# A feed-forward up-projection by seven block products, with the gated activations kept in DRAM until a separate down-projection

## The chip, the cores and the metric

One core of a Trainium2 chip runs one encoder layer (token mixer, cross attention, gated feed-forward network) on 2048 tokens of width 1024. The metric is the device time of one execution in microseconds (us), and runs are compared by their median. TensorE (PE) multiplies matrices into PSUM, VectorE (DVE), ScalarE (ACT) and GpSimd (POOL) work on elements, and SyncE (SP) issues the DMAs. Each engine takes its instructions in the order of the program and waits on semaphores for the others.

## The reference, cut to what matters

```python
def conv_glu_ffn(h, w_up, conv_w, conv_b, w_down):
    u = h @ w_up
    gate, val = u[..., :D_FF], u[..., D_FF:]
    gate = causal_dwconv(gate, conv_w, conv_b)
    return (jax.nn.silu(gate) * val) @ w_down

x = x + mem_cross_attn(h, memn, x_wq[l], x_wkv[l], x_wo[l])
h = rmsnorm(x, norm_ffn[l])
x = x + conv_glu_ffn(h, f_up[l], f_conv_w[l], f_conv_b[l], f_down[l])
return rmsnorm(x, norm_final)
```

`D_FF` is 2816. The convolution runs along the tokens and has three taps. All arrays are fp32.

## The kernel before, in words

After the token mixer comes a block in which a scheduler sets the order of each engine's instructions. It works on two halves of 1024 tokens, and each half is two blocks of 512 tokens (`NB` = 2, `TB` = 512). For a half: `out_proj` and `scores` for both blocks, then `attn_out` for both, which leaves the residual `x` and the scaled operand `h3` of eight tiles (128 rows of the model width by 512 tokens) in SBUF, then `ffn`.

An fp32 product is made of three matmuls. A value is split into a high part (a cast to the rounded type fp32r, on ScalarE) and a low part (value minus high part, on GpSimd or VectorE), and a product is high x high, high x low and low x high. So each raw weight tile costs one cast and one subtraction per 512 columns before it can be used. `load_w` does that into `whl`, from the two buffers of `wraw`.

`ffn` loops over `f`, the 22 tiles of 128 feed-forward rows. For each `f` it multiplies the gate weights with `h3` of both token blocks (24 matmuls each), applies the scale of the normalization (`bc3`), the three taps (ScalarE's L1385 and twice L1387 on VectorE) and the activation (L1390, L1391, L1392), then does the same with the value weights, multiplies (L1398) and splits the result into `act`. After every second `f` (`GRP`), it multiplies the two `act` tiles of each block with the down weights and adds to the residual in SBUF (L1417). After the last `f` of a half comes the final normalization (`finish`). `ahead` puts the next half's first `out_proj` before the last down-projection group.

The buffers that matter: `kt` has 32 tiles of 128x1024 (4 KB a row), `kq` 7 of the same size, `T` 6 and `TQ` 4 of 128x512, PSUM 7 banks (`PD`). A buffer is taken again when its last reader is done.

Of the kernel before, what the change touches and what calls it, by code (L numbers as in the profile page):

```python
# [13 lines left out]
F32 = mybir.dt.float32  # L14
# [42 lines left out]
def tile_hybrid_encoder(ctx: ExitStack, tc: tile.TileContext, t_in: dict, out: bass.AP, stage: str = "all"):  # L57
# [1132 lines left out]
    x1_dram = dram.tile([KT, P, S], F32, name="x1_dram")  # L1190
    align(tp, 320)
# [133 lines left out]
    def attn_out(s_, between):  # L1325
        x2, h3, acc = [], [], None
        for d in range(KT):
            w = [pre_split(vo_dram[d, q], (P, 2, 4, P), "wvo") for q in range(2)]
            w = [(t_[:, 0], t_[:, 1]) for t_ in w]
            if d % 2 == 0:  # L1330
                xx = K4((P, 2, TB), "x2", F32)
            x = xx[:, d % 2, :]
# [16 lines left out]

    def attention(st, toks):  # L1350
        pr = None
        for b in range(NB):
# [14 lines left out]
    GRP = 2  # L1367

    def ffn(tok0, st, xs, h3, ahead):
        acts = [[] for _ in range(NB)]  # L1370
        wds = []
        for f in range(NFF):
            wg = load_w(t_in["f_up"][f])
            us = []
            for b in range(NB):
                ps = PD()
                dense(ps, wg, h3[b])
                if f == 0 and b == 0:
                    norm_bc(st[NB - 1])
                    bc3 = [s_["bc3"] for s_ in st]  # L1380
                gt_ = T((P, TB + 2), "gt_")
                nc.gpsimd.tensor_copy(gt_[:, 0:2], fcar[f])
                nc.vector.tensor_tensor(gt_[:, 2:], ps, bc3[b], ALU.mult)
                u = T(name="fu")
# [8 lines left out]
                us.append(u)  # L1393
            wv = load_w(t_in["f_up"][NFF + f])
            for b in range(NB):
                ps = PD()
                dense(ps, wv, h3[b])
                nc.vector.scalar_tensor_tensor(us[b], us[b], 0.5, ps, ALU.mult, ALU.mult)  # L1398
                a = K4((P, 2, TB), "act")
                split_sbuf(a[:, 0, :], a[:, 1, :], us[b])  # L1400
                acts[b].append(a)
            wds.append(split_w(load_raw(t_in["f_down"][f]), [P, 8, P], kq, ("kq", "kq"), 7))
            if f == NFF - 1:
                ahead()
            if len(wds) == GRP:
                end = f == NFF - 1
                bcf = []
                order = [(d, b) for b in range(NB) for d in range(KT)] if end else [(d, b) for d in range(KT) for b in range(NB)]
                for d, b in order:
                    ps = PD(name="dps")  # L1410
                    for g in range(GRP):
                        a = acts[b][g]
                        hi, lo = wds[g]
                        nc.tensor.matmul(ps, hi[:, d, :], a[:, 0, :], start=(g == 0), stop=False)  # L1414
                        nc.tensor.matmul(ps, hi[:, d, :], a[:, 1, :], start=False, stop=False)  # L1415
                        nc.tensor.matmul(ps, lo[:, d, :], a[:, 0, :], start=False, stop=(g == GRP - 1))  # L1416
# [126 lines left out]
```

## Time and profile before

| | |
|---|---|
| median of 3 runs | 3452.25 us (3449.77 to 3452.82) |
| the profiled execution: time, span | 3447.24 us, 3445.5 us |
| PE busy | 3321.1 us (96%), 17388 matmuls |
| DVE, ACT, POOL busy | 1902.4, 1170.9, 1177.1 us (55, 34, 34%) |
| mean granted TensorE clock | 0.987 |
| chain that ended last: PE, DVE, DMA | 80, 9, 3% |

The span runs from the first to the last instruction. Matmuls overlap, so the pitch of a matmul is read from starts, not from its own length of 389 ns. A row of the timeline gives start, length, engine, line, operation, output and inputs, how many instructions it merges, and in brackets the idle time before it and what ended it.

### The profile page before, as it was taken

The numbers are of one execution on the slowest core, as the hardware profiler recorded it, in microseconds if no ns is written. First come the engines' busy times: TensorE is split into PE (matmuls) and PEld (weight loads), VectorE is DVE, ScalarE is ACT, GpSimd is POOL, SyncE is SP. The second block draws the span as 40 slices with busy tenths as digits, with TensorE's granted clock in tenths as the row PEclk, the third lists the DMA queues.
The fourth block names the chain that finished last, engine by engine and source line by source line (L and its number), as shares of the span: only waits on it lengthen the run. The fifth ranks groups of instructions, "written<-read, shape, count | busy, mean of one in ns | idle before, by whom it ended". The sixth has DMA issues, their size and how long they took to land.

```text
span 3445.5 us, 47020 instructions
## 1 busy us (share of the span) xinstructions
PE 3321.1 (96%) x17388; PEld 2728.8 (79%) x17388; DVE 1902.4 (55%) x3916; ACT 1170.9 (34%) x2307; POOL 1177.1 (34%) x1254
## 2 busy tenths in 40 slices
PE   6899999999999989899999999999999999999997
PEld 4777787788778778688888888887888888888886
DVE  5887777777777775343244444444643344444445
ACT  5445433543443345442221221222432212212213
POOL 5333121211211123531343443444531434434433
PEclk9999999999999999999999999999999999999998
DMA  6555444544444447766411111112656211111111
GB/s 208 207 181 180 142 142 129 178 133 137 147 130 133 131 127 242 261 208 205 139 58 40 49 55 43 44 55 95 223 178 227 96 37 56 55 37 52 53 43 55
DMA packets 225701, 423.19 MB, mean 123 GB/s; under 512 B 79552, under 2 KB 111424, under 8 KB 225472
## 3 DMA queue, kind: packets, MB, share of 16 engines
q1 hardware_dynamic: 221248, 418.10, 36.9%
q8 instruction: 137, 2.24, 0.3%
q10 hardware_dynamic: 4224, 2.10, 0.2%
q14 instruction: 92, 0.75, 0.1%
HBM read 342.44 MB, written 77.66 MB: 122 GB/s over the span
## 4 chain that ended last, share of the span: by engine, by line
PE 80%; DVE 9%; DMA 3%; ACT 3%; issue 3%; POOL 2%; SPq 0%; DVEq 0%; ACTq 0%; POOLq 0%
PE pd L173 13%; PE pd L176 12%; PE pd L175 12%; PE pd L147 12%; PE dps L1416 4%; PE dps L1415 4%; PE dps L1414 4%; PE qy L147 2%; PE sc L1295 2%; PE sc L1297 2%; PE sc L1296 2%; DVE pr L719 1%; PE pab L147 1%; DVE pr L739 1%; PE p L147 1%
## 5 line engine op out<-in xcount | busy, mean ns | idle before, releaser
L147 PE MATMUL pd<-hA,whl 128*128 128x512 f32 x2976 | 813.0, 410 | 17.1 <-ACT whl L121 8.4
L147 PEld LDWEIGHTS pd<-hA,whl 128*128 128x128 f32 x2976 | 534.8, 191 | 120.8 <-ACT whl L121 9.4
L176 PE MATMUL pd<-h,whl 128*128 128x512 f32 x1408 | 547.9, 389 | 0.0
L173 PE MATMUL pd<-h,whl 128*128 128x512 f32 x1408 | 547.9, 389 | 0.0
L175 PE MATMUL pd<-h,whl 128*128 128x512 f32 x1408 | 547.7, 389 | 0.0
L124 POOL TENSOR_TENSOR whl<-wraw,whl 128x512 fp32r<-128x512 f32 x313 | 417.5, 1345 | 327.6 <-ACT whl L121 318.8
L1417 DVE TENSOR_TENSOR x<-dps,x 128x512 f32<-128x512 f32 x352 | 235.6, 689 | 224.3 <-PE dps L1416 222.3
L121 ACT CAST whl<-wraw 128x512 fp32r<-128x512 f32 x334 | 204.0, 621 | 317.8 <-PE pd L176 271.8
L175 PEld LDWEIGHTS pd<-h,whl 128*128 128x128 f32 x1408 | 264.3, 188 | 54.9
L176 PEld LDWEIGHTS pd<-h,whl 128*128 128x128 f32 x1408 | 264.3, 188 | 54.8
L173 PEld LDWEIGHTS pd<-h,whl 128*128 128x128 f32 x1408 | 264.3, 188 | 54.8
L1416 PE MATMUL dps<-act,wlo 128*128 128x512 f32 x704 | 271.0, 390 | 0.0
L1415 PE MATMUL dps<-act,whi 128*128 128x512 f32 x704 | 270.6, 389 | 0.0
L1414 PE MATMUL dps<-act,whi 128*128 128x512 f32 x704 | 260.9, 389 | 0.1
L1398 DVE SCALAR_TENSOR_TENSOR fu<-fu,pd 128x512 f32<-128x512 f32 x88 | 60.6, 688 | 217.3 <-PE pd L176 169.8
L1414 PEld LDWEIGHTS dps<-act,whi 128*128 128x128 f32 x704 | 132.1, 188 | 28.2 <-DVE x L1417 0.8
L1415 PEld LDWEIGHTS dps<-act,whi 128*128 128x128 f32 x704 | 132.2, 188 | 27.5
L1416 PEld LDWEIGHTS dps<-act,wlo 128*128 128x128 f32 x704 | 132.2, 188 | 27.4
L1217 POOL TENSOR_TENSOR sq<-sq 128x512 f32<-128x512 f32 x56 | 73.4, 1311 | 220.6 <-ACT sq L1214 220.6
L1392 POOL TENSOR_TENSOR fu<-fu,bcs 128x512 f32<-128x512 f32 x88 | 114.2, 1298 | 97.2 <-DVE fu L1391 95.7
L1391 DVE SCALAR_TENSOR_TENSOR fu<-fth,fu 128x512 f32<-128x512 f32 x88 | 87.9, 998 | 67.6 <-ACT fth L1390 67.6
L147 PE MATMUL qy<-UV,F 128*66 128x64 f32 (+1 forms) x1024 | 124.1, 244 | 0.0
(918 smaller groups left out, 6082.8 us busy)
## 6 DMA issues: line engine op xcount, KB each, us to landing
whl<-w_split SPq DMA_DIRECT2D x186, 512.0 KB
wraw<-f_up SPq DMA_DIRECT2D x88, 512.0 KB
wqk<-qk_dram SPq DMA_DIRECT2D x64, 512.0 KB
wvo<-vo_dram SPq DMA_DIRECT2D x64, 512.0 KB
w_split<-whl SPq DMA_DIRECT2D x62, 512.0 KB
wraw<-f_down SPq DMA_DIRECT2D x44, 512.0 KB
wraw<-w_out SPq DMA_DIRECT2D x32, 512.0 KB
wraw<-w_in SPq DMA_DIRECT2D x31, 512.0 KB
```

The source lines that it names most:

```text
L121: nc.scalar.copy(t_[:, 0], r_)
L124: (nc.vector if dve else nc.gpsimd).tensor_tensor(t_[:, 1], r_, t_[:, 0].bitcast(F32), ALU.subtract)
L147: nc.tensor.matmul(out_, lhsT, rhs, **kw)
L173: nc.tensor.matmul(ps, hi[:, k % 4, :], a[:, 0, :n], start=(k == 0), stop=False)
L175: nc.tensor.matmul(ps, hi[:, k % 4, :], a[:, 1, :n], start=False, stop=False)
L176: nc.tensor.matmul(ps, lo[:, k % 4, :], a[:, 0, :n], start=False, stop=(k == last and not late))
L1391: nc.vector.scalar_tensor_tensor(u, th, 1.0, u, ALU.add, ALU.mult)
L1392: nc.gpsimd.tensor_tensor(u, u, bc3[b], ALU.mult)
L1414: nc.tensor.matmul(ps, hi[:, d, :], a[:, 0, :], start=(g == 0), stop=False)
L1415: nc.tensor.matmul(ps, hi[:, d, :], a[:, 1, :], start=False, stop=False)
L1416: nc.tensor.matmul(ps, lo[:, d, :], a[:, 0, :], start=False, stop=(g == GRP - 1))
L1417: nc.vector.tensor_tensor(xs[b][d], ps, xs[b][d], ALU.add)
```

## The change

The up-projection of one `f` is a product of 2x2 blocks: rows are gate and value weights, the inner dimension is two halves of the model width (g1, g2, v1, v2), columns are the two token blocks. Eight block products of 12 matmuls become seven. For that, the weights are combined (s1 = v1 + v2, s2 = s1 - g1, s3 = v1 - g1, s4 = g2 - s2) and so are the operands (t1 to t4, once per half), all before they are split, and the products are combined after (u2, p7, c21). The gated result is written to `act_dram`. A separate `ffn_down` then reads it back, splits it, and sums all 22 `f` in PSUM for four output tiles at a time; `f_down` is read per token block. The residual goes through `x2_dram`.

```diff
+    def resplit(t_, eng, raw=None):
+        raw = t_[:, 1].bitcast(F32) if raw is None else raw
+        nc.scalar.copy(t_[:, 0], raw)
+        eng.tensor_tensor(t_[:, 1], raw, t_[:, 0].bitcast(F32), ALU.subtract)
...
+    def attn_out(s_, o, B, between):
...
+            nc.sync.dma_start(x2_dram[d, :, s_["tok"]], x)
...
+                nc.vector.tensor_tensor(t2r, b22r, t1r, ALU.subtract)
+                nc.vector.scalar_tensor_tensor(t3r, xl, gl, b22r, ALU.mult, ALU.subtract)
+                for n, r_ in (("t1", t1r), ("t3", t3r), ("t2", t2r), ("22", b22r)):
+                    B[n].append(K4((P, 2, TB), "h3"))
+                    resplit(B[n][-1], nc.vector if n in ("t1", "t3") else nc.gpsimd, r_)
...
+    def ffn_up(hf, st, B):
...
+            a11 = plain(whl("a11"), g1, nc.gpsimd)
+            s1, s3, s2, s4 = [KQ((P, 2, H, P), "ws") for _ in range(4)]
...
+            nc.gpsimd.tensor_tensor(s1r, v1, v2, ALU.add)
+            nc.vector.tensor_tensor(s3r, v1, g1, ALU.subtract)
+            nc.vector.tensor_tensor(s2r, s1r, g1, ALU.subtract)
+            nc.gpsimd.tensor_tensor(s4r, g2, s2r, ALU.subtract)
+            resplit(s1, nc.gpsimd, s1r)
+            resplit(s3, nc.vector, s3r)
+            resplit(s2, nc.vector, s2r)
+            a12 = plain(whl("a12"), g2, nc.gpsimd)
+            resplit(s4, nc.gpsimd, s4r)
+            a22 = plain(whl("a22"), v2, nc.gpsimd)
...
+            X, Z, W, Y = [PD(name="pd") for _ in range(4)]
+            prod(X, a11, "11")
+            p1 = kept(X, "p1")
+            prod(Z, s1, "t1")
+            p5 = kept(Z, "p5")
+            prod(W, s3, "t3")
+            p7 = kept(W, "p7")
+            prod(Y, s2, "t2")
...
+            nc.vector.tensor_tensor(u2, Y, p1, ALU.add)
+            nc.gpsimd.tensor_tensor(p7, p7, p5, ALU.add)
...
+                if b == 0:
+                    nc.vector.tensor_tensor(gt_[:, 2:], X, bc3[b], ALU.mult)
+                else:
+                    nc.vector.tensor_tensor(gt_[:, 2:], Z, u2, ALU.add)
+                    nc.vector.tensor_tensor(gt_[:, 2:], gt_[:, 2:], bc3[b], ALU.mult)
...
+            prod(X, a12, "21", True)
+            gate(0)
+            prod(Z, s4, "22", True)
+            gate(1)
+            prod(W, a22, "t4", True)
+            nc.vector.tensor_tensor(c21, W, u2, ALU.add)
+            nc.vector.tensor_tensor(p7, p7, u2, ALU.add)
+            for b, c in enumerate((c21, p7)):
+                nc.vector.scalar_tensor_tensor(us[:, b], us[:, b], 0.5, c, ALU.mult, ALU.mult)
+                nc.sync.dma_start(act_dram[hf, f, b], us[:, b])
...
+    def ffn_down(hf, ahead):
...
+            for dh in range(2):
...
+                for f in range(NFF):
+                    if dh == 0:
+                        a = K4((P, 2, TB), "act")
+                        nc.sync.dma_start(a[:, 1].bitcast(F32), act_dram[hf, f, b])
+                        resplit(a, nc.vector)
...
+                    w, raw = KQ((P, 2, H, P), "wd"), T((P, H, P), "wdr")
+                    nc.sync.dma_start(raw, t_in["f_down"][f][:, dh * H:(dh + 1) * H])
+                    resplit(w, nc.gpsimd, raw)
...
+            bc = bcast_sbuf(acc)
+            for d in range(KT):
+                nc.vector.scalar_tensor_tensor(xs[d], xs[d], V("norm_final", d), bc, ALU.mult, ALU.mult)
+                nc.sync.dma_start(out[d * P:(d + 1) * P, ts_], xs[d])
```

POOL in the feed-forward loop before, one `f` (L124, L105 and L187 are low parts of up weights, down weights and activations):

```order
L1382 COPY gt__19802<-fcar_15467 128x2
L1392 TENSOR_TENSOR fu_19560<-fu_19560,bcs_17607 128x512
L105 TENSOR_TENSOR wlo_19921<-wraw_19917,whi_19919 128x1024
L187 TENSOR_TENSOR act_19603<-fu_19523,act_19603 128x512
L124 TENSOR_TENSOR whl_19853<-wraw_19851,whl_19853 128x512
L124 TENSOR_TENSOR whl_19854<-wraw_19851,whl_19854 128x512
L187 TENSOR_TENSOR act_19632<-fu_19560,act_19632 128x512
L1388 COPY fcar_15467<-gt__19802 128x2
L124 TENSOR_TENSOR whl_19925<-wraw_19923,whl_19925 128x512
L1382 COPY gt__19839<-fcar_15467 128x2
L1392 TENSOR_TENSOR fu_19805<-fu_19805,bcs_17297 128x512
L124 TENSOR_TENSOR whl_19926<-wraw_19923,whl_19926 128x512
```

and in the loop of the change, one `f` (L1331 is the low part of any split; a11, a12, a22 and ws are weights; sr is a raw combination; ahead of these rows stand `p7 + p5` and a copy of `fcar`):

```order
L1331 TENSOR_TENSOR a22_19325<-wraw_19299,a22_19325 128x512
L1468 COPY fcar_15469<-gt__19244 128x2
L1417 TENSOR_TENSOR sr_19308<-wraw_19299 128x512
L1459 COPY gt__19267<-fcar_15469 128x2
L1331 TENSOR_TENSOR ws_19304<-sr_19308,ws_19304 128x512
L1420 TENSOR_TENSOR sr_19309<-wraw_19297,sr_19309 128x512
L1472 TENSOR_TENSOR fu_19230<-fu_19230,bcs_17312 128x512
L1468 COPY fcar_15469<-gt__19267 128x2
L1331 TENSOR_TENSOR a11_19460<-wraw_19456,a11_19460 128x512
L1331 TENSOR_TENSOR ws_19307<-sr_19309,ws_19307 128x512
L1331 TENSOR_TENSOR a12_19479<-wraw_19456,a12_19479 128x512
L1472 TENSOR_TENSOR fu_19230<-fu_19230,bcs_17781 128x512
```

The low parts of seven weight tiles, two combinations and the products with `bc3` stand in one row of POOL, for `f`, the next one and the one after it, and the down weights have left the loop.

DVE in the loop before, one `f`, without the additions of the down-projection:

```order
L1383 TENSOR_TENSOR gt__19520<-pd_19495,bcs_17297 128x512
L1387 SCALAR_TENSOR_TENSOR fu_19523<-gt__19520,vec_68,fu_19523 128x512 x2
L1391 SCALAR_TENSOR_TENSOR fu_19523<-fth_19528,fu_19523 128x512
L1383 TENSOR_TENSOR gt__19557<-pd_19532,bcs_17607 128x512
L1387 SCALAR_TENSOR_TENSOR fu_19560<-gt__19557,vec_68,fu_19560 128x512 x2
L1391 SCALAR_TENSOR_TENSOR fu_19560<-fth_19565,fu_19560 128x512
L1398 SCALAR_TENSOR_TENSOR fu_19523<-fu_19523,pd_19577 128x512
L1398 SCALAR_TENSOR_TENSOR fu_19560<-fu_19560,pd_19606 128x512
```

and in the loop of the change (ahead of these stand u2 = Y + p1 (L1451), p7 + u2 (L1480) and the first gate start from X (L1461)):

```order
L1418 TENSOR_TENSOR sr_19308<-wraw_19299,wraw_19297 128x512
L1467 SCALAR_TENSOR_TENSOR fu_19230<-gt__19244,vec_68,fu_19230 128x512 x2
L1463 TENSOR_TENSOR gt__19267<-pd_19170,u2_19227 128x512
L1419 TENSOR_TENSOR sr_19309<-sr_19308,wraw_19297 128x512
L1471 SCALAR_TENSOR_TENSOR fu_19230<-fth_19251,fu_19230 128x512
L1464 TENSOR_TENSOR gt__19267<-gt__19267,bcs_17781 128x512
L1331 TENSOR_TENSOR ws_19305<-sr_19308,ws_19305 128x512
L1331 TENSOR_TENSOR ws_19306<-sr_19309,ws_19306 128x512
L1467 SCALAR_TENSOR_TENSOR fu_19230<-gt__19267,vec_68,fu_19230 128x512 x2
L1479 TENSOR_TENSOR c21_19231<-pd_19171,u2_19227 128x512
L1482 SCALAR_TENSOR_TENSOR fu_19230<-fu_19230,c21_19231 128x512
L1471 SCALAR_TENSOR_TENSOR fu_19230<-fth_19275,fu_19230 128x512
```

Where ten operations stood for each `f`, beside eight additions of L1417, there are 18 now, and the weight combinations of the next `f` (sr, ws) stand between the steps of this one's gate.

ACT at the passage from the last `f` of a half to the down-projection, which did not exist before (act are activations read back, fth the last tanh, wd the down weights):

```order
L1330 CAST act_21419<-act_21419 128x512
L1330 CAST act_21440<-act_21440 128x512
L1330 CAST act_21461<-act_21461 128x512
L1470 ACTIVATE fth_21183<-fu_21138 128x512
...
L1330 CAST act_21611<-act_21611 128x512
L1330 CAST act_21632<-act_21632 128x512
L1330 CAST wd_21213<-wdr_21214 128x512
L1330 CAST wd_21234<-wdr_21235 128x512
```

21 casts of `act` stand ahead of the first cast of `wd`, eight of them behind the last tanh; SP's loads of them stand in the same order.

## Rows read from the trace of the kernel before

**Rows 1.** Windows: length; busy us (xcount) of PE, PEld, DVE, ACT, POOL; PEclk, DMA.
```profile
1694.00:2390.00 696.00, 696.00 (x3080) 576.53 (x3079) 293.53 (x382) 164.10 (x242) 304.99 (x284) 1.00 0.16 52
2697.00:3423.00 726.00, 726.00 (x3217) 601.58 (x3216) 311.64 (x414) 182.49 (x271) 305.75 (x285) 1.00 0.14 45
```

**Rows 2.** Timeline of TensorE: first matmuls of the first two gate products.
```profile
1693.62 0.39 PE L173 MATMUL pd<-h,whl 128*128 128x512 f32 x1
...
1699.06 0.39 PE L173 MATMUL pd<-h,whl 128*128 128x512 f32 x1
```

**Rows 3.** Page, groups: one of three up, one of three down lines.
```profile
L173 PE MATMUL pd<-h,whl 128*128 128x512 f32 x1408 | 547.9, 389 | 0.0
...
L1414 PE MATMUL dps<-act,whi 128*128 128x512 f32 x704 | 260.9, 389 | 0.1
```

**Rows 4.** Timeline of DVE, one gate of each token block.
```profile
1898.61 1.54 DVE L1387 SCALAR_TENSOR_TENSOR fu<-gt__18930,vec,fu 128x512 f32<-128x512 f32 x2 [0.94 <-ACT fu L1385]
1900.93 1.35 DVE L1391 SCALAR_TENSOR_TENSOR fu<-fth,fu 128x512 f32<-128x512 f32 x1 [0.78 <-ACT fth L1390]
1902.42 0.69 DVE L1383 TENSOR_TENSOR gt__18967<-pd,bcs 128x512 f32<-128x512 f32 x1
1904.12 2.11 DVE L1387 SCALAR_TENSOR_TENSOR fu<-gt__18967,vec,fu 128x512 f32<-128x512 f32 x2 [1.02 <-ACT fu L1385]
1907.00 0.69 DVE L1391 SCALAR_TENSOR_TENSOR fu<-fth,fu 128x512 f32<-128x512 f32 x1 [0.76 <-ACT fth L1390]
```

**Rows 5.** Timeline of POOL in the same stretch.
```profile
1900.44 1.29 POOL L124 TENSOR_TENSOR whl<-wraw,whl 128x512 fp32r<-128x512 f32 x1 [2.46 <-ACT whl L121]
1901.68 0.65 POOL L1382 COPY gt__18967<-fcar 128x2 f32<-128x2 f32 x1
1902.37 1.29 POOL L1392 TENSOR_TENSOR fu<-fu,bcs 128x512 f32<-128x512 f32 x1
...
1905.44 0.18 POOL L1382 COPY gt__19084<-fcar 128x2 f32<-128x2 f32 x1
```

**Rows 6.** Timeline of DVE, end of the first half (final scaling).
```profile
2476.11 6.37 DVE L1431 TENSOR_TENSOR x<-x,bcs 128x512 f32<-128x512 f32 x5 [2.93 <-ACT bcs L1237]
```

**Rows 7.** Timeline of POOL, same stretch.
```profile
2476.16 5.17 POOL L1431 TENSOR_TENSOR x<-x,bcs 128x512 f32<-128x512 f32 x3 [3.87 <-ACT bcs L1237]
```

**Rows 8.** Groups by line, 1694 to 2390: count, busy us, mean ns, idle before.
```profile
L124 POOL TENSOR_TENSOR whl<-wraw,whl 128x512 fp32r<-128x512 f32 x87 | 111.6, 1292 | 53.5 <-ACT whl L121 53.4
...
L1392 POOL TENSOR_TENSOR fu<-fu,bcs 128x512 f32<-128x512 f32 x44 | 57.1, 1298 | 46.2 <-DVE fu L1391 45.4
...
L121 ACT CAST whl<-wraw 128x512 fp32r<-128x512 f32 x87 | 54.2, 624 | 112.8 <-PE pd L176 112.8
...
L1398 DVE SCALAR_TENSOR_TENSOR fu<-fu,pd 128x512 f32<-128x512 f32 x43 | 29.6, 688 | 103.7 <-PE pd L176 77.6 <-POOL act L187 23.7 <-POOL fu L1392 2.4
```

**Rows 9.** Timeline of DVE in a down-projection group.
```profile
1943.22 2.48 DVE L1417 TENSOR_TENSOR x<-dps,x 128x512 f32<-128x512 f32 x4 [2.03 <-PE dps L1416]
```

**Rows 10.** Timeline of SP's queue: a down weight load is issued.
```profile
1904.93 0.33 SPq L96 DMA_DIRECT2D wraw<-f_down  x1
```

**Rows 11.** Timeline of ACT: the cast that waits for that load.
```profile
1908.36 1.05 ACT L101 CAST whi<-wraw 128x1024 fp32r<-128x1024 f32 x1 [1.39 <-DMA wraw<-f_down]
```

**Rows 12.** Windows around a stop of TensorE, columns as in rows 1.
```profile
2392.00:2395.00 3.00, 1.00 (x4) 0.86 (x5) 1.19 (x2) 2.81 (x6) 2.29 (x2) 1.00 0.60 230
2395.00:2401.00 6.00, 4.74 (x12) 3.17 (x11) 5.82 (x4) 2.59 (x5) 6.00 (x5) 0.50 0.22 87
```

**Rows 13.** Timeline of DVE at the program's end.
```profile
3422.98 0.69 DVE L1417 TENSOR_TENSOR x<-dps,x 128x512 f32<-128x512 f32 x1
...
3431.20 0.15 DVE L182 TENSOR_SCALAR rstd<-ssps 128x4 f32<-128x4 f32 x1
3435.22 6.30 DVE L1431 TENSOR_TENSOR x<-x,bcs 128x512 f32<-128x512 f32 x5 [3.87 <-ACT bcs L1237]
```

**Rows 14.** Timeline of ACT at the program's end.
```profile
3434.60 0.58 ACT L1237 COPY bcs<-bcB 128x512 f32<-128x512 f32 x1 [9.17 <-PE bcB L1232]
```

More of the change, by code (lines that the diff above doesn't have):

```diff
@@ L1366, in tile_hybrid_encoder, with plain, prod, kept @@
     fcar = [fcars[:, 4 * f:4 * f + 2] for f in range(NFF)]
[L1367 to L1371, printed above, removed]
+    def ffn_up(hf, st, B):
+        H = KT // 2
+        whl = lambda name: wpool.tile([P, 2, H, P], FR, tag="whl", name=name, bufs=WB)
+        bc3 = None
         for f in range(NFF):
[L1373 to L1380, printed above, removed]
+            rg, rv = load_raw(t_in["f_up"][f]), load_raw(t_in["f_up"][NFF + f])
+            g1, g2, v1, v2 = rg[:, :H], rg[:, H:], rv[:, :H], rv[:, H:]
+            def plain(t_, src, eng):
+                resplit(t_, eng, src)
+                return t_
+            a11 = plain(whl("a11"), g1, nc.gpsimd)
+            s1, s3, s2, s4 = [KQ((P, 2, H, P), "ws") for _ in range(4)]
+            s1r, s3r, s2r, s4r = [t_[:, u] for t_ in [K4((P, 2, H, P), "sr", F32) for _ in range(2)] for u in range(2)]
+            nc.gpsimd.tensor_tensor(s1r, v1, v2, ALU.add)
[8 more added lines that the diff above has]
+            a22 = plain(whl("a22"), v2, nc.gpsimd)
+            def prod(ps, w, b, more=False):
+                for k in range(H):
+                    nc.tensor.matmul(ps, w[:, 0, k, :], B[b][k][:, 0, :], start=(k == 0 and not more), stop=False, skip_group_check=True)
+                    nc.tensor.matmul(ps, w[:, 0, k, :], B[b][k][:, 1, :], start=False, stop=False, skip_group_check=True)
+                    nc.tensor.matmul(ps, w[:, 1, k, :], B[b][k][:, 0, :], start=False, stop=(k == H - 1), skip_group_check=True)
+            def kept(ps, name):
+                t_ = TQ(name=name)
+                nc.scalar.copy(t_, ps)
+                return t_
+            X, Z, W, Y = [PD(name="pd") for _ in range(4)]
[6 more added lines that the diff above has]
+            prod(Y, s2, "t2")
+            if bc3 is None:
+                norm_bc(st[NB - 1])
+                bc3 = [s_["bc3"] for s_ in st]
+            u2 = T(name="u2")
+            nc.vector.tensor_tensor(u2, Y, p1, ALU.add)
+            nc.gpsimd.tensor_tensor(p7, p7, p5, ALU.add)
+            us = K4((P, 2, TB), "fu", F32)
+            c21 = T(name="c21")
+            def gate(b):
+                u = us[:, b]
@@ L1403, in ffn @@
[L1403 to L1416, printed above, removed]
-                    nc.vector.tensor_tensor(xs[b][d], ps, xs[b][d], ALU.add)
-                    if end:
-                        acc = sum_sq(None if d == 0 else acc, xs[b][d], d, True)
-                        nc.scalar.activation(xs[b][d], xs[b][d], AF.Copy, scale=V("norm_final", d))
-                        if d == KT - 1:
-                            bcf.append(bcast_sbuf(acc))
-                for b in range(len(bcf)):
-                    finish(tok0 + b * TB, xs[b], bcf[b])
-                wds = []
-                acts = [[] for _ in range(NB)]
```

105 lines of the change are left out of this document (72 added, 33 removed).

## The prediction

> **What bounds the kernel now.** I read the table by stretches first. In both feed-forward stretches [rows 1] TensorE is busy for the whole of the time at granted clock 1.00, while VectorE is busy 42%, ScalarE 24% and GpSimd 44%: TensorE sets the time there. Its pitch comes from two starts in the timeline [rows 2]: 24 matmuls (8 K tiles, three each) lie between 1693.62 and 1699.06, so one 128x512 matmul takes 0.2267 us. One f is 96 matmuls of the up-projection and 48 of the down-projection [rows 3] (3 x 1408 / 44 and 3 x 704 / 44), or 21.76 + 10.88 us.
>
> **What is removed.** 84 matmuls take the place of 96: 19.04 us instead of 21.76 per f, 2.72 us less, 119.7 us over 44 f. That would be the gain if TensorE kept setting the time. The 48 of the down-projection stay.
>
> **What is added, and where it is paid.** The DVE and POOL rows printed above, one f of the changed loop each, are the term that decides. POOL now has 10 full-size operations per f (before: 8, and one of 1024 columns, but over 32.6 us) and 4 tiny copies; DVE has 18, of which four read PSUM (u2, the two gate starts L1461 and L1463, c21) and 14 read two SBUF tensors. In a busy-time sum all this fits: 18 x 0.69 to 0.75 = 12.7 us of DVE and 10 x 1.30 + 0.7 = 13.7 us of POOL [rows 4, 5, 8] against 19.04.
>
> It doesn't fit if the two engines get in each other's way, and the trace shows that they do. The gate's last VectorE operation reads two SBUF tensors and takes 1.35 us when POOL's split began before it (1900.44, 1.29 long), and the two taps take 2.11 instead of 1.54 for the same reason [rows 4, 5]; POOL's tiny copy takes 0.65 when VectorE holds the way and 0.18 when not. VectorE operations with a PSUM operand are not touched: L1383 takes 0.69 wholly under POOL's 1.29, and L1398 has a mean of 688 ns [rows 4, 5, 8]. Where both engines run back to back on SBUF tensors, POOL's three operations take 5.17 us, 1.72 each, with one VectorE operation passed between two of them [rows 6, 7]; alone they would take 1.30 and 0.69. So a POOL operation and a VectorE operation on SBUF together cost 1.72, nearly their sum.
>
> The Trainium skill (SBUF — State Buffer, section "Who interferes with whom") says the same as a rule: a VectorE instruction with two SBUF inputs and a GpSimd instruction that reads SBUF contend, and the later one blocks fully. Our trace agrees on which operations contend, and differs a little on the price: 1.72 a pair where two full blocks would be 1.99. By the row's price the sum below is 3531 us, by the rule's it would be 3666.
>
> Per f of the changed loop: ten pairs x 1.72 = 17.2; the other four VectorE operations at their pitch alone, 0.62 (2.48 / 4) [rows 9] = 2.5; four tiny copies x 0.18 = 0.7. That is 20.4 us during which the way to SBUF is taken, more than TensorE's 19.04. To this come the places where the printed order lets neither engine use it. I walked the order by hand and find three of about 0.7: at L1461 (DVE is on PSUM; POOL's copy waits for its result), at L1463 (POOL waits for ScalarE's cast of s1), and at c21, where POOL waits for the next a11. That last wait is new: both raw tiles (two buffers) are in use until s4r is made, the next load goes out only then, and a load of this size takes 3.43 us to its reader [rows 10, 11] plus a 0.62 cast [rows 8], while POOL has only one operation to fill in. So **one block takes 20.4 + 2.1 = 22.5 us**, 0.7 more than the 21.76 it replaces. I take 22.5; the bounds are 20.4 (no holes) and 25.7 (14 operations of 0.69 to 0.75, ten of 1.30 and the copies, 23.6, nothing overlapped, plus the holes).
>
> TensorE then stops for 3.5 us in each block. Before, a stop of 2.0 us was followed by 6 us at clock 0.50, the lower of its two levels (1.2 GHz) [rows 12]; that costs up to 3 us of matmuls a block, 19.04 + 3 = 22.0, still under 22.5, so I add nothing for it.
>
> **The ends of the loop.** Before, the gate products follow the attention output without a stop [rows 2]. Now seven sets of operands have to exist first. From the last row of the attention output, DVE has 19 two-SBUF operations up to the low part of s2 of the first f (the printed rows show its tail), POOL ten in the same time: 10 x 1.72 + 9 x 0.62 = 22.8, plus 0.7 for the addition and about 2 for the last matmuls: the first u2 stands at 25.5 us, where TensorE's own work would have brought it at 10.9. At the other end, ScalarE's order has 21 casts of act tiles ahead of the first cast of down weights, and the last tanh in the middle of them. That tanh waits for VectorE: counting from the end E of the last product, gate start by E - 2.0, three more operations by E + 0.1, four low parts and a tap by E + 3.6, three and a tap by E + 6.4, tanh E + 7.1, eight casts of 0.62 and the weight cast: E + 12.7. TensorE waits that long, and pays about 2.8 for the clock. From the last u2 that is 8.2 + 12.8 + 2.8 = 23.8. So a half's up-projection takes 25.5 + 21 x 22.5 + 23.8 = 521.8 us where 22 x 21.76 = 478.7 stood: **+43.1 per half, +86.2 in all**. If prefetch hid both ends, it would be 60 less.
>
> **Costed at nothing.** The down-projection keeps TensorE's 2.72 us per f and output half; beside it run one POOL operation, one VectorE operation (1.72 together) and two casts (1.24), and 512 KB of loads, 193 GB/s; the cover is TensorE's 2.72. The writes of x2 add 256 KB per 5.44 us to the attention output; the sub-microsecond SP issue [rows 10] is covered by five or more queued weight loads. Extra operand work in the second block's output stage is 6 two-SBUF operations and 4 of POOL per 10.9 us (8.1 us).
>
> **The tail gets shorter.** Before, the last addition starts at 3422.98, the normalizer's first step waits behind five multiplications until 3431.20, its copy ends at 3435.18, the second five end at 3441.52, and the stores at 3445.5 [rows 13, 14]: 22.5 us after the last matmul. Now one block's chain is left: 0.4 + 0.7 + 0.6 + 0.7 to the sums, 4.0 for the normalizer, 8 x 0.62 = 5.0, and 4.0 for the stores: 15.4, so -7.1.
>
> **The sum.** 3447.2 (the profiled execution: span 3445.5 plus 1.7 around it) + 86.2 - 7.1 = 3526. The median of the runs before is 5 us above that execution, so I predict 3531 as a median.
>
> **Rivals.** (1) *TensorE stays the bound* (the faster side). The two engines' operations interleave so that the shared way costs under 19 us. For it: the sum of busy times fits, and an operation that meets a free way takes its 0.69 (1907.00 in [rows 4]). Against: ten POOL operations leave hardly a gap. Per half 25.5 + 21 x 19.04 + 23.8 = 449.1, in all 3386. The sign turns where 25.5 + 21T + 23.8 = 478.7 + 3.6, at a block of T = 20.6 us. (2) *The weight load paces the block.* Two raw tiles of 512 KB go out together after s4r; if the first reader sees them after 5 us instead of 3.4, a11, s4's low part and the last tanh behind them on ScalarE move by up to as much: T = 23.6 to 24.1, 3577 to 3600. For it: the queue is in order behind the act stores. Against: single loads of 3.43. (3) *No overlap at all on the shared way*: T = 25.7, 3666. Against: the 1.72 of [rows 7]. The Trainium skill's rule of that section, taken strictly, would give this.
>
> **How the numbers follow.** Forecast, a block of 21.3 to 24.1 us (3481 to 3600): 0.68. Holes nearly filled, 20.4 to 21.3 (3443 to 3481): 0.12, a quarter of it below the old time and a quarter within 0.2% of it (7 us, about what a measurement of this kernel can tell). TensorE bound (3380 to 3443): 0.12. Above 3600: 0.08. The range 3442 to 3600 leaves out 0.2. Faster 0.15, same 0.03, slower 0.82; the forecast's own range is 3481 to 3600.
>
> **What would show it.** Right: in the up-projection TensorE's share falls to about 85% with granted clock under 1.0, u2 (L1451) recurs every 22 to 23 us, taps and low parts on VectorE show means near 1.2 us instead of 0.75, POOL operations near 1.6, and c21 stays at 0.69. A stop of 20 us or more stands on TensorE at each end of the loop in sum. Wrong: u2 recurring every 19 us with TensorE full would mean that the operations slip past each other; a block above 24 us with POOL waiting on the load would mean rival 2.

## The result and the profile after

The changed kernel takes 3554.68 us (median of 4 runs, 3552.81 to 3561.95) against 3452.53 in the same job: ratio 1.0301, 95% interval 1.0283 to 1.0319. It is slower, as predicted, by 102 us where 79 were forecast. The profiled execution has a span of 3560.2 us, 114.7 more than before; it was the longest of its four, and the one profiled before, with 3447.24 us, was shorter than the four of this job, which makes this difference larger than that of the medians. Of the 114.7, 6.8 lie in the unchanged mixer ahead of 1416 us. The page's first part:

```profile
PE 3281.8 (92%) x16860; PEld 2654.7 (75%) x16860; DVE 2298.4 (65%) x4104; ACT 1355.2 (38%) x2703; POOL 1581.8 (44%) x1486
```

TensorE has 528 matmuls less, 119.7 us at the old pitch, and is busy only 39.3 us less; VectorE and GpSimd are busy 396 and 405 us more. The windows of the first half show where that falls. They are, in this order, the start of the up-projection, its 21 blocks, its end, the first three groups of the down-projection, and its last group (most of the next output projection stands between these two); columns as in [rows 1], the last one GB/s.

```profile
1705.00:1745.00 40.00, 21.23 (x79) 16.44 (x78) 28.50 (x29) 14.94 (x26) 29.60 (x20) 0.74 0.20 58
1745.00:2195.00 450.00, 423.96 (x1778) 334.35 (x1777) 406.86 (x379) 169.76 (x294) 367.19 (x295) 0.98 0.22 75
2195.00:2230.00 35.00, 15.37 (x60) 11.78 (x59) 28.78 (x37) 21.09 (x36) 21.28 (x16) 0.71 0.89 313
2230.00:2413.00 183.00, 176.28 (x766) 145.18 (x765) 44.22 (x54) 57.39 (x97) 85.62 (x64) 0.97 0.45 147
...
2456.00:2540.00 84.00, 63.10 (x272) 52.20 (x273) 15.89 (x21) 25.64 (x43) 40.62 (x32) 0.88 0.52 165
```

In the blocks (second row) VectorE is busy 90%, GpSimd 82% and TensorE 94%; before, TensorE was the engine that was never idle [rows 1]. One block on VectorE, from u2 to u2 (timeline):

```profile
1915.31 0.68 DVE L1451 TENSOR_TENSOR u<-pd,p 128x512 f32<-128x512 f32 x1
1916.09 1.14 DVE L1480 TENSOR_TENSOR p<-p,u 128x512 f32<-128x512 f32 x1
...
1918.78 2.27 DVE L1467 SCALAR_TENSOR_TENSOR fu<-gt__19085,vec,fu 128x512 f32<-128x512 f32 x2 [0.36 <-POOL fcar L1468]
...
1921.57 0.68 DVE L1419 TENSOR_TENSOR sr<-sr,wraw 128x512 f32<-128x512 f32 x1
1922.17 0.68 DVE L1471 SCALAR_TENSOR_TENSOR fu<-fth,fu 128x512 f32<-128x512 f32 x1
1922.78 1.78 DVE L1464 TENSOR_TENSOR gt__19108<-gt__19108,bcs 128x512 f32<-128x512 f32 x1
1924.47 3.46 DVE L1331 TENSOR_TENSOR ws<-sr,ws 128x512 fp32r<-128x512 f32 x2
1927.86 2.44 DVE L1467 SCALAR_TENSOR_TENSOR fu<-gt__19108,vec,fu 128x512 f32<-128x512 f32 x2
1930.23 0.68 DVE L1479 TENSOR_TENSOR c<-pd,u 128x512 f32<-128x512 f32 x1
...
1935.10 1.76 DVE L1482 SCALAR_TENSOR_TENSOR fu<-fu,p 128x512 f32<-128x512 f32 x1 [1.40 <-POOL fu L1472]
1936.79 0.68 DVE L1451 TENSOR_TENSOR u<-pd,p 128x512 f32<-128x512 f32 x1
```

and on GpSimd in the same stretch:

```profile
1918.43 1.29 POOL L1417 TENSOR_TENSOR sr<-wraw 128x512 f32<-128x512 f32 x1
1919.67 0.65 POOL L1459 COPY gt__19108<-fcar 128x2 f32<-128x2 f32 x1
1922.39 1.61 POOL L1331 TENSOR_TENSOR ws<-sr,ws 128x512 fp32r<-128x512 f32 x1 [2.07 <-ACT ws L1330]
1923.96 1.74 POOL L1420 TENSOR_TENSOR sr<-wraw,sr 128x512 f32<-128x512 f32 x1
1925.65 1.73 POOL L1472 TENSOR_TENSOR fu<-fu,bcs 128x512 f32<-128x512 f32 x1
1927.33 0.65 POOL L1468 COPY fcar<-gt__19108 128x2 f32<-128x2 f32 x1
...
1933.78 1.28 POOL L1472 TENSOR_TENSOR fu<-fu,bcs 128x512 f32<-128x512 f32 x1 [0.63 <-DVE fu L1471]
```

The block takes 21.48 us (1915.31 to 1936.79). The reader should look at the lengths. While GpSimd waits (2.07 ahead of 1922.39), VectorE's operations take 0.68. From 1922.78 on both engines run back to back, and one VectorE operation and one GpSimd operation pass in 1.69 to 1.70 together (starts 1922.78, 1924.47 and 1927.86; 1923.96 and 1925.65). Where nothing holds it up, a VectorE operation is followed by the next after 0.60 and a GpSimd operation after 1.24 (1921.57 to 1922.17; 1918.43 to 1919.67), in sum 1.84. So each waits for nearly all of the other, as in [rows 6, 7], and the wait shows as a longer operation: the busy shares above contain it. The Trainium skill (SBUF — State Buffer, section "Who interferes with whom") says that of such a pair the later one blocks; the trace agrees up to about 0.15 us a pair. The product c21, which reads PSUM, keeps its 0.68.

The account of the 114.7 us, from starts in the trace, against the matmuls of the kernel before at their pitch of 0.2267 (478.7 per half for the up-projection):

| stretch | half 0 | half 1 | against the pitch |
|---|---|---|---|
| attention output's end to first u2 | 40.1 | 39.2 | |
| 21 blocks | 450.0 | 448.4 | |
| last u2 to first down matmul | 21.4 | 20.4 | |
| up-projection in all | 511.5 | 508.0 | +62.1 |
| down-projection beyond its 1056 matmuls (and 192 of the next output projection) at 0.2267 | 39.0 | 19.7 | +58.7 |
| last matmul to the end | | 15.9 (22.7 before) | -6.8 |
| mixer; the rest | | | +6.8; -6.1 |

The rest has two parts. The two feed-forward halves before, with the next output projection, took 773.2 and 720.8 us where the pitch gives 761.6 and 718.1, so 14 us of losses had been there already. And the attention stages ahead of the two up-projections, which now also write x2 and make more operands, are 8 us longer in sum (4.5 and 3.9); what in them takes longer was not taken apart.

### The profile page after: what moved, and what is told of

It reads as the page before. It is cut to its first block, busy times and chain, and to the rows that moved or that the text cites. A ratio compares the mean times of both kernels' runs of the same rounds, so it can differ in the third digit from the quotient of the medians.

```text
span 3560.2 us, 48232 instructions
## 1 busy us (share of the span) xinstructions
PE 3281.8 (92%) x16860; PEld 2654.7 (75%) x16860; DVE 2298.4 (65%) x4104; ACT 1355.2 (38%) x2703; POOL 1581.8 (44%) x1486
## 5 line engine op out<-in xcount | busy, mean ns | idle before, releaser
L1430 PE MATMUL pd<-h,ws 128*128 128x512 f32 x704 | 293.3, 417 | 59.0 <-ACT ws L1330 59.0
L1502 PE MATMUL dps<-act,wd 128*128 128x512 f32 x704 | 281.8, 400 | 66.7 <-ACT wd L1330 66.7
L1331 POOL TENSOR_TENSOR wd<-wdr,wd 128x512 fp32r<-128x512 f32 x176 | 235.6, 1355 | 194.6 <-ACT wd L1330 192.4
L124 POOL TENSOR_TENSOR whl<-wraw,whl 128x512 fp32r<-128x512 f32 x137 | 187.0, 1375 | 253.4 <-ACT whl L121 245.3
L1431 PE MATMUL pd<-h,ws 128*128 128x512 f32 x704 | 284.8, 405 | 0.0
L1503 PE MATMUL dps<-act,wd 128*128 128x512 f32 x704 | 280.7, 399 | 0.0
L1432 PE MATMUL pd<-h,ws 128*128 128x512 f32 x704 | 271.2, 406 | 0.0
L1504 PE MATMUL dps<-act,wd 128*128 128x512 f32 x704 | 268.4, 392 | 1.1 <-POOL wd L1331 1.1
L1430 PEld LDWEIGHTS pd<-h,ws 128*128 128x128 f32 x704 | 137.7, 196 | 117.8 <-ACT ws L1330 94.9
L1331 POOL TENSOR_TENSOR a<-wraw,a 128x512 fp32r<-128x512 f32 x132 | 210.4, 1594 | 2.2 <-ACT a L1330 2.2
L1502 PEld LDWEIGHTS dps<-act,wd 128*128 128x128 f32 x704 | 135.7, 193 | 98.0 <-ACT wd L1330 69.7
L1430 PE MATMUL pd<-h,a 128*128 128x512 f32 x528 | 206.7, 391 | 0.0
L1431 PE MATMUL pd<-h,a 128*128 128x512 f32 x528 | 206.0, 390 | 0.0
L1432 PE MATMUL pd<-h,a 128*128 128x512 f32 x528 | 205.8, 390 | 0.0
L1331 POOL TENSOR_TENSOR ws<-sr,ws 128x512 fp32r<-128x512 f32 x88 | 146.9, 1670 | 88.4 <-ACT ws L1330 88.4
L1432 PEld LDWEIGHTS pd<-h,ws 128*128 128x128 f32 x704 | 137.1, 195 | 42.3 <-POOL ws L1331 11.3
L1508 DVE TENSOR_TENSOR x<-dps,x 128x512 f32<-128x512 f32 x32 | 21.7, 690 | 214.0 <-PE dps L1504 214.0
```

What stands on the lines that cost most here:

```text
L124: (nc.vector if dve else nc.gpsimd).tensor_tensor(t_[:, 1], r_, t_[:, 0].bitcast(F32), ALU.subtract)
L1331: eng.tensor_tensor(t_[:, 1], raw, t_[:, 0].bitcast(F32), ALU.subtract)
L1430: nc.tensor.matmul(ps, w[:, 0, k, :], B[b][k][:, 0, :], start=(k == 0 and not more), stop=False, skip_group_check=True)
L1431: nc.tensor.matmul(ps, w[:, 0, k, :], B[b][k][:, 1, :], start=False, stop=False, skip_group_check=True)
L1432: nc.tensor.matmul(ps, w[:, 1, k, :], B[b][k][:, 0, :], start=False, stop=(k == H - 1), skip_group_check=True)
L1502: nc.tensor.matmul(pss[i], hi[:, i, :], a[:, 0, :], start=(f == 0), stop=False)
```

## Experiments

Each changes one thing in the changed kernel, if nothing else is said; "less" and "more" compare with its 3554.68 us, and ratios with the kernel before in the same job. Theory S is the prediction's: in a block VectorE and GpSimd are bound by the way to SBUF that they share, and TensorE waits for them.

**1. p7 from PSUM.**

```diff
-            p7 = kept(W, "p7")
...
-            nc.gpsimd.tensor_tensor(p7, p7, p5, ALU.add)
+            p7 = TQ(name="p7")
+            nc.vector.tensor_tensor(p7, W, p5, ALU.add)
```

> p7 is read straight from PSUM by VectorE (p7 = W + p5) instead of being copied by ScalarE and added by GpSimd (L1452). Theory S (the way to SBUF that VectorE and GpSimd share paces the block of 21.4 us): the final L1482 and L1480 no longer meet a GpSimd operation (1.76 and 1.14 become 0.68 each), and the added VectorE operation of 0.68 fits into the 1.4 us in which VectorE waits for the gate product: 1.1 to 1.5 us less a block, 50 to 65 us less in all, 3490 to 3505. Rival L (the load of the raw weights paces the block): no change, 3550 to 3560. Rival T (TensorE sets the block, its matmuls being slower than 0.2267): no change.

Measured: 3514.79 us, ratio to before 1.0192 (1.0172 to 1.0212), 40 us less than the changed kernel. The block falls from 21.48 to 20.5. VectorE's timeline:

```profile
1896.67 0.69 DVE L1482 SCALAR_TENSOR_TENSOR fu<-fu,p 128x512 f32<-128x512 f32 x1 [1.41 <-POOL fu L1472]
1897.28 0.68 DVE L1452 TENSOR_TENSOR p<-pd,p 128x512 f32<-128x512 f32 x1
1897.88 0.68 DVE L1450 TENSOR_TENSOR u<-pd,p 128x512 f32<-128x512 f32 x1
1898.60 0.69 DVE L1480 TENSOR_TENSOR p<-p,u 128x512 f32<-128x512 f32 x1
```

L1482 loses 1.07 and L1480 0.45, because the GpSimd operation that they met is gone. The added operation costs its pitch of 0.60: it did not go into the wait of 1.41, as I had expected. That makes -0.92 a block, 40 in 44 blocks: the mechanism is S, but the gain is smaller than expected, and the time lies outside the expected 3490 to 3505.

**2. The raw up weights loaded once.**

```diff
-            rg, rv = load_raw(t_in["f_up"][f]), load_raw(t_in["f_up"][NFF + f])
+            if f == 0:
+                rg, rv = load_raw(t_in["f_up"][f]), load_raw(t_in["f_up"][NFF + f])
```

> The raw up weights are loaded once per half, for the first f, and all 22 blocks use them (left out: 84 of the 88 loads, so the output is that of other weights). Theory S: no operation of VectorE or GpSimd goes away and they seldom wait for the load: at most 0.3 us a block, 3540 to 3560. Rival L: the wait for the next raw tiles is gone, a block falls to 19.0 to 20.0, 3460 to 3495.

Measured: 3558.94 us, ratio 1.0312 (1.0295 to 1.0329), and the blocks stay at 21.5. The load does not pace the block, and rival 2 of the prediction (L in the expectation) falls.

**3. Three low parts off GpSimd.**

```diff
-                resplit(t_, eng, src)
+                nc.scalar.copy(t_[:, 0], src)
+                nc.scalar.copy(t_[:, 1], src)
```

> The low parts of a11, a12 and a22 are no longer made by GpSimd; ScalarE writes a copy of the raw values in their place (left out: the three subtractions, so the low parts are wrong). GpSimd keeps seven full-size operations a block instead of ten, ScalarE gets three more of 0.62. Theory S: GpSimd's 4.8 us less sets VectorE free as well, the block falls to TensorE's 19.0 to 19.6 us, 3455 to 3480 in all. Rival T: no change, since TensorE has the same matmuls. Rival L can't be told from S here: the raw tiles come free earlier too.

Measured: 3462.04 us, ratio 1.0031 (1.0018 to 1.0045). The blocks take 19.3 us. A window over 14 of them:

```profile
1800.00:2070.00 270.00, 269.81 (x1188) 222.17 (x1187) 230.69 (x253) 137.76 (x238) 183.66 (x154) 1.00 0.24 82
```

TensorE is busy for 269.81 of 270 us. With three operations fewer on GpSimd and as many on VectorE, the block is TensorE's again, so its 84 matmuls were not what held the blocks of 21.5. The raw tiles come free earlier here too, but experiment 2 has shown that this is worth nothing.

**4. Eight products, the separate down-projection kept.** `attn_out` and the products as before the change, the result to `act_dram`:

```diff
+            wv = load_w(t_in["f_up"][NFF + f])
+            for b in range(NB):
+                ps = PD()
+                dense(ps, wv, B[b])
+                nc.vector.scalar_tensor_tensor(us[:, b], us[:, b], 0.5, ps, ALU.mult, ALU.mult)
+                nc.sync.dma_start(act_dram[hf, f, b], us[:, b])
```

> Undoes the seven products alone: gate and value as eight block products with the operands of the kernel before, while the gated activations still go through DRAM to the separate down-projection, and x2 too. Theory A (the separate down-projection costs only its start, as predicted: a stop of 12.8 and 2.8 for the clock at each half, a tail 7.1 shorter): 3470 to 3485. Theory B (the stops that the changed kernel's trace shows after the up-projection, 19 and 16 at the starts, 21 before the last group of the first half, two near 5, and the lower clock around them, all belong to the separate down-projection): 70 us of stops and some 10 of clock, less 7: 3510 to 3530; the seven products would then cost only 25 to 45 of the 102.

Measured: 3498.75 us, ratio 1.0140 (1.0118 to 1.0162), between the two theories. The up-projection is TensorE bound again (480.5 us in half 0), and the stop at its end is 4.3 us in half 0 and 0.9 in half 1, but the stops of 20.4 before the last group and of 4.7 and 4.6 at the second token block are there. So by medians the separate down-projection, with the way through DRAM, costs 47 us, and the seven products the other 56; the long stop between the projections appears only with the seven products.

**5. Down weights first.**

```diff
             gate(1)
+            if f == NFF - 1:
+                early[:] = [first_wd(g) for g in range(3)]
             prod(W, a22, "t4", True)
...
+                    if b == 0 and dh == 0 and f < 8:
+                        w = early[f] if f < len(early) else first_wd(f)
```

The cause to be tested is seen in the changed kernel on ScalarE. Between the last product (TensorE's last matmul starts at 2197.16) and the first weight cast stand 21 casts of activations, eight of them in the first of these rows; the last row is TensorE, which waits for that cast:

```profile
2203.98 4.71 ACT L1330 CAST act<-act 128x512 fp32r<-128x512 f32 x8
2210.12 0.63 ACT L1470 ACTIVATE fth<-fu 128x512 f32<-128x512 f32 x1 [1.42 <-DVE fu L1467]
...
2215.69 1.96 ACT L1330 CAST wd<-wdr 128x512 fp32r<-128x512 f32 x3
...
2216.36 0.80 PE L1502 MATMUL dps<-act,wd 128*128 128x512 f32 x1 [18.82 <-ACT wd L1330]
```

> The first eight tiles of down weights of a half are loaded through the raw-tile buffers, the first three of them before the last product of the up-projection, so that their casts stand ahead of the 21 casts of gated activations on ScalarE. Theory O (the stop of 18.8 and 16.2 us between the two projections comes from that order): the stops shrink to under 5 us, 22 to 32 us less with the clock, 3522 to 3533. Rival M (the stop is bound by memory: the activations' way through DRAM and the loads at 313 GB/s in that stretch): the stop stays above 12 us, under 10 us less.

Measured: 3524.82 us, ratio 1.0219 (1.0192 to 1.0246), 30 us less. TensorE's first down matmuls:

```profile
2189.22 0.79 PE L1518 MATMUL dps<-act,wd 128*128 128x512 f32 x1 [4.93 <-ACT act L1330]
```

This stop is 4.93 and that of half 1 is 4.87, where the kernel with the change alone had 18.82 and 16.20. It was the order; rival M falls. The edit moves the weights ahead of the activations in two queues at once, the casts on ScalarE and the loads on SyncE, where the first load of a down weight had been issued at 2210.04, behind the loads of the 21 activations; how much each queue is worth was not told apart.

**6. The next output projection later.** `ahead()` is called behind the 18 first steps of the last group, not before them.

```diff
-                if lastg:
-                    ahead()
...
+                if lastg:
+                    ahead()
                 for i in range(H):
                     for f in range(NFF - tail, NFF):
```

> The next half's first output projection is emitted after the 18 first steps of the last output group instead of before them. Theory C (the stop of 20.9 us before that group comes from 32 buffers that hold 22 activation tiles, x2, the projection's inputs and its outputs at the same time, so that its outputs, and behind them on SyncE the down weights, wait): the stop goes, 20 to 25 us less, 3530 to 3535. Rival D (the down weights themselves are late): the stop moves in front of the first 18 steps, under 8 us less.

Measured: 3536.01 us, ratio 1.0249 (1.0232 to 1.0267), 19 us less, 1 us outside the expected range. Behind the 4.9 us at the start of the second token block no stop over 2.4 us is left in that half: the place of the projection made the stop. In the changed kernel two queues show how. ScalarE writes no output tile of that projection until 2451, when TensorE's last 24 matmuls of it (from 2450.37) begin to set its inputs free. By the program, 22 activation tiles, two tiles of x2 and the eight inputs hold all 32 buffers until then; that the buffers are the reason is argued, since no run had more of them.

```profile
2450.62 0.62 ACT L121 CAST whl<-wraw 128x512 fp32r<-128x512 f32 x1 [2.11 <-PE pd L176]
2451.25 2.08 ACT L1268 ACTIVATE h<-x,vec 128x512 fp32r<-128x512 f32 x3
```

On SyncE the down weights come only behind the last of the projection's stores:

```profile
2472.84 0.33 SPq L1270 DMA_DIRECT2D x_dram<-x  x1
2473.22 8.16 SPq L1518 DMA_DIRECT2D wdr<-f_down  x7
```

**7. t4 and the second normalizer behind the first gate.**

```diff
             gate(0)
+            if f == 0:
+                late_t4(B)
+                norm_bc(st[NB - 1])
```

> At the start of the up-projection the four t4 operands (needed only by the last product) and the second block's normalizer are emitted behind the first gate instead of ahead of the first f's weight sums. Theory Q (the 39.9 us from the attention output to the first u2 are VectorE's and GpSimd's queue of operand work, 12 and 4 operations of it t4's, and a TensorE that waits for the normalizer in order): the first u2 comes 12 to 20 us earlier, part of it is paid back in the first block: 16 to 36 us less in all, 3519 to 3539. Rival R (the raw weights or the last rows of the attention output set the start): under 8 us less.

Measured: 3560.30 us, ratio 1.0317 (1.0297 to 1.0337): no gain. (The edit also takes the buffers of these operands from another pool.) The first two u2:

```profile
1726.97 0.69 DVE L1449 TENSOR_TENSOR u<-pd,p 128x512 f32<-128x512 f32 x1 [5.42 <-PE pd L1433]
...
1759.84 0.68 DVE L1449 TENSOR_TENSOR u<-pd,p 128x512 f32<-128x512 f32 x1
```

The first u2 stands 26.6 us after the attention output instead of 40.1, and the first block takes 32.9 instead of 19.8: 13.5 won, 13.0 given back. The time is in rival R's range, but not for its reason, since the first u2 did move. VectorE and GpSimd have the operand work to do, now or one block later, and theory Q had expected only a part of it to come back.

**8. All four (1, 5, 6, 7).**

> p7 from PSUM, down weights first, next output projection later and late t4 together. If the causes are separate stretches, the savings add: 40 measured for the first, 27 and 22 and 25 expected for the others: 3435 to 3455, about the time of the kernel before. If what one stop gives back is waited for at the next place instead (theory G, one queue of VectorE and GpSimd work behind all of them), the sum is half: 3480 to 3500.

Measured: 3470.79 us, ratio 1.0056 (1.0038 to 1.0074). Neither expected range was met, because late t4 gave nothing. The savings measured singly, 40 + 30 + 19 - 6, give 83, and 84 came out: the stretches are separate causes.

**9. One GpSimd operation more.**

```diff
+            nc.gpsimd.tensor_tensor(p1, p1, u2, ALU.add)
             prod(W, a22, "t4", True)
```

> The changed kernel with one more GpSimd operation per block, p1 = p1 + u2 in SBUF, 128x512, whose result nobody reads (44 of them; the output is unchanged). Theory S (the way to SBUF shared with VectorE paces the block): 1.3 to 1.8 us more a block, 57 to 79 in all, 3610 to 3635. Rival B (only GpSimd's own busy time counts: 17.5 us of a block of 21.4, so that 3.9 are free): less than 0.3 a block, 3555 to 3570.

Measured: 3597.06 us, ratio 1.0437 (1.0422 to 1.0451), 42 us more by medians and 47 by the ratios; a block takes 22.4. Neither expected number was met, but rival B is out: GpSimd had 3.9 us to spare, and the operation cost 0.9. VectorE's timeline says where:

```profile
1921.21 1.81 DVE L1481 TENSOR_TENSOR p<-p,u 128x512 f32<-128x512 f32 x1
1922.94 0.68 DVE L1461 TENSOR_TENSOR gt__19093<-pd,bcs 128x512 f32<-128x512 f32 x1
1923.54 1.18 DVE L1418 TENSOR_TENSOR sr<-wraw 128x512 f32<-128x512 f32 x1
1924.64 2.42 DVE L1467 SCALAR_TENSOR_TENSOR fu<-gt__19093,vec,fu 128x512 f32<-128x512 f32 x2
```

Against the block shown above, this L1481 (there L1480) takes 0.67 more, L1418 0.50 and the taps 0.15, and the wait of 0.36 ahead of the taps is gone: 0.96, near the 0.9 of the block. So this GpSimd operation cost the block what it took from VectorE. That the missing part of it (1.29 unhindered) fell into GpSimd's own holes (1.28 and 2.07 there) is the likely reason for the lower price, which no run isolates.

**10. Three edits (1, 5, 6).**

> p7 from PSUM, down weights first and next output projection later, without late t4. The late t4 alone changed nothing: the first u2 came 13.2 us earlier and the first block took 13.1 longer, so the operand work is the bound there and not its order. So this should be the time of all four together, or 5 us less: 3464 to 3472. If late t4 did help in that combination: 3475 to 3485.

Measured: 3467.65 us, ratio 1.0056 (1.0042 to 1.0070), the ratio of all four, as expected: late t4 adds nothing here either.

**11. Splits kept for half 1**, on top of the three:

```diff
+                for q, t_ in enumerate((a11, s1, s3, s2, a12, s4, a22)):
+                    nc.sync.dma_start(u_split[f, q], t_.bitcast(F32))
+            else:
+                a11, s1, s3, s2, a12, s4, a22 = tiles = [
+                    KQ((P, 2, H, P), "ws") if q in (1, 2, 3, 5) else whl("a") for q in range(7)]
+                for q, t_ in enumerate(tiles):
+                    nc.sync.dma_start(t_.bitcast(F32), u_split[f, q])
```

> The three edits, and the seven split weight tiles of every f are written to DRAM in the first half and loaded ready-made in the second, so that half 1 has no GpSimd or VectorE work on weights (8 and 5 operations fewer a block) and 3.67 MB of loads a block instead of 1.05; half 0 has 3.67 MB of stores more. Theory S: blocks of half 1 fall from 20.5 to 19.0 to 19.3 us, TensorE's own time, the first u2 of half 1 comes up to 8 us earlier, half 0 keeps 20.5: 27 to 40 us less than the three edits, 3425 to 3440, faster than the kernel before. Rival M (the transfers, 218 GB/s in half 1 and in half 0, pace the block instead): blocks of 20.5 or more in half 1 or longer ones in half 0, no gain or a loss, 3465 to 3500.

Measured: 3415.97 us, ratio 0.9913 (0.9899 to 0.9927), the first version that is faster than the kernel before, by 0.9%. The windows of half 0 and half 1:

```profile
1795.00:2097.00 302.00, 291.82 (x1236) 225.64 (x1235) 272.40 (x278) 112.85 (x194) 240.92 (x192) 1.00 0.68 258
2784.00:3088.00 304.00, 304.00 (x1343) 251.73 (x1342) 165.12 (x240) 63.02 (x96) 64.85 (x96) 1.00 0.63 221
```

The same matmuls take 20.5 us a block in half 0, where VectorE (90%) and GpSimd (80%) are full, and 19.0 in half 1, where GpSimd is busy 21% and TensorE all the time. The transfers, 258 and 221 GB/s (last column), cost nothing here. It is 52 us less than the three edits, more than the 27 to 40 expected: the blocks give 21 x 1.5 = 32, the first u2 comes 12 us earlier in half 1 (27.8 after the attention output instead of 40.1) and 5 in half 0, and the stop at half 1's up-projection end, 4.9, is gone.

**12. x1 one row ahead**, on top of 11:

```diff
-            x = T(name="x2")
-            nc.sync.dma_start(x, x1_dram[d, :, s_["tok"]])
+            x = nx
+            if i + 1 < KT:
+                nx = load_x(rows[i + 1])
```

It tests what the changed kernel shows on SyncE at the end of the attention output:

```profile
1709.35 0.32 SPq L1344 DMA_DIRECT2D x_dram<-x  x1
1709.77 0.37 SPq L1340 DMA_DIRECT2D x<-x_dram  x1
```

and on VectorE, whose last addition waits for that load until 9.3 us after the last matmul (the up-projection's first starts at 1704.87):

```profile
1714.22 0.69 DVE L1343 TENSOR_TENSOR x<-pd,x 128x512 f32<-128x512 f32 x1 [0.46 <-DMA x<-x_dram]
```

> The kernel with the splits kept, and in the attention output the load of each row's x1 is emitted one row ahead, so that on SyncE it no longer stands behind the store of x2 of the row before. Theory X (that order makes the last addition late: 9.3 us after the attention output's last matmul in the changed kernel, 12.7 in half 1 of the kernel with kept splits, 2.7 in its half 0): the last addition of half 1 follows within 1 to 3 us, the first u2 of half 1 comes 7 to 11 us earlier, half 0 gains up to 3: 7 to 14 us less, 3402 to 3409. Rival Q (the operand work of VectorE and GpSimd sets the start, whenever x1 arrives): under 4 us less, 3412 to 3417.

Measured: 3398.70 us, ratio 0.9849 (0.9828 to 0.9870), 17 us less than experiment 11, more than the 7 to 14 expected. VectorE in half 1:

```profile
2701.64 0.69 DVE L1352 TENSOR_TENSOR x<-pd,x 128x512 f32<-128x512 f32 x1 [0.37 <-PE pd L176]
...
2717.28 0.68 DVE L1483 TENSOR_TENSOR u<-pd,p 128x512 f32<-128x512 f32 x1
```

The last addition waits for TensorE again, and the first u2 stands 15.9 us after the attention output, 12 earlier than without the edit; in half 0 it is 29.4 instead of 33.2. This version is 1.5% faster than the kernel before.

## Why the prediction was right, and where its terms were off

Sign and mechanism held: the block is set by the way to SBUF that VectorE and GpSimd share (experiments 1, 3, 9 and 11), not by TensorE (rival 1) and not by the load (rival 2). The pieces of the sum:

- *One block, 22.5 us: too long by 1.0.* Measured 21.48, in 21 blocks and two halves 47 us less than forecast. The pair of 1.72 held (1.69 to 1.70). Of the three holes, those at L1461 and L1463 are there on GpSimd (1.28 and 2.07 us), but VectorE works in the second. The third, at c21 for the next raw tiles, doesn't exist: c21 starts right behind the taps, GpSimd runs on, and without the loads nothing changed (experiment 2). What does make VectorE wait, 1.40 for the last gate product, I had not seen. (The text ahead of the prediction puts the low parts of all seven weight tiles on GpSimd; five stand there and two on VectorE, as its rows show and as the count of ten takes them.)
- *The start of the loop, 25.5 us: 14 too short.* Measured 40.1 and 39.2. The operand work came out as summed: VectorE's 19 operations behind the last addition, t4's among them, take 22.5 us (1714.83 to 1737.33) where 22.8 stood. Two other terms were off. The first is the last row's addition, which starts 9.3 us after the matmuls; the sum has 0.7 for the addition and no wait. I had costed x2's stores at nothing, because weight loads are queued ahead; but each row's x1 load stands behind the store of the row before on SyncE, and experiment 12 took that wait away in the version with kept splits. The second is the 2 us for the last matmuls: VectorE waits 7.61 for them, because TensorE, which takes its matmuls in order, had stood for the second normalizer until 1725.00 and then for split weights, and works at a low clock (0.74 in the first window above):

```profile
1744.95 0.69 DVE L1451 TENSOR_TENSOR u<-pd,p 128x512 f32<-128x512 f32 x1 [7.61 <-PE pd L1432]
```

- *The end, 23.8 us from the last u2: nearly right.* The start of the down-projection is 21.4 and 20.4 after it, the clock's loss not counted, which falls behind the start. The cause that was named, activations ahead of the first down weights, is shown by experiment 5, as an order in ScalarE's and SyncE's queues together.
- *The down-projection, costed at nothing: the largest error, 58.7 us against the pitch* (at most 14 of them had been lost before as well). I had looked at its throughput (loads, splits), which does fit, and not at the starts of its groups. TensorE stops there for 2.02, 4.71 and 20.93 us in half 0, and in half 1 for 4.60 (the first block's normalizer) and twice 2.01:

```profile
2347.76 0.79 PE L1502 MATMUL dps<-act,wd 128*128 128x512 f32 x1 [4.71 <-ACT wd L1330]
...
2476.90 0.80 PE L1502 MATMUL dps<-act,wd 128*128 128x512 f32 x1 [20.93 <-ACT wd L1330]
```

After such a stop its clock is low. The window behind the first of these two rows:

```profile
2348.00:2352.00 4.00, 4.00 (x10) 3.13 (x11) 0.43 (x1) 2.15 (x4) 4.00 (x3) 0.50 0.70 211
```

It is the lower of the two levels, 0.50, as in [rows 12]: ten matmuls in 4 us. The stops named are 27.7 of the 39.0 us in half 0 and 8.6 of the 19.7 in half 1; the rest is the lower clock and stops under 2 us, which I did not take apart.
- *The tail, -7.1: right* (-6.8).

That the sum came within 24 us of the medians is in part luck, because its errors cancel: the up-projection was overrated by 24 us (47 too much for the blocks and 6 for the ends, against 28 too little for the starts) and the down-projection underrated by 59.

Of the signs named under "What would show it", these came: GpSimd's means are 1.60 to 1.68 for the low parts (1.6 said), the second gate's taps have a mean of 1.20 (1.2 said), and c21 keeps 0.68 (0.69 said). Others were off in size: u2 recurs every 21.5 us (22 to 23 said), low parts on VectorE take 1.75 (1.2 said), and TensorE's share in the blocks is 94%, not 85%: at a clock of 0.98 part of the lost time is in slower matmuls.

## What to carry to other kernels

A saving on the engine that sets the time is worth only what the next engine leaves: price the work that the saving needs on the engines that will do it, as pairs where two engines hold each other up, before counting matmuls. When a fused loop is cut in two, every group of the new loop has a start of its own; follow each queue (casts on ScalarE, loads behind stores on SyncE, full buffer pools) at each of them, since throughput says nothing about starts. And work that an engine must do anyway is not saved by moving it: make it fewer operations, let it read PSUM, or do it once and load the result.

## What was not expected of the hardware

GpSimd can be held up for much longer than one operation of VectorE, while in the loop the two took turns. At the end of the up-projection one of its products, 1.28 us unhindered, took 5.28, while VectorE ran activation splits and a product from 2214.22 to 2218.5 with no gap. What decides between the two cases no run shows.

```profile
2214.22 1.88 DVE L1331 TENSOR_TENSOR act<-act 128x512 fp32r<-128x512 f32 x3
2216.03 0.68 DVE L1482 SCALAR_TENSOR_TENSOR fu<-fu,c 128x512 f32<-128x512 f32 x1
2216.63 1.88 DVE L1331 TENSOR_TENSOR act<-act 128x512 fp32r<-128x512 f32 x3
...
2214.37 5.28 POOL L1472 TENSOR_TENSOR fu<-fu,bcs 128x512 f32<-128x512 f32 x1 [8.57 <-DVE fu L1471]
```

Transfers of 3.67 MB of weights a block (experiment 11) did not slow TensorE in half 1, which was busy all the time at granted clock 1.00, nor the block of half 0, which took 20.5 us with the stores and without them.
